# The S5 mixer's tables prepared by GpSimd instead of the vector engine

## The chip, the cores and the metric

The kernel runs on one core of a Trainium2 chip. The metric is the device time of one execution in microseconds (us). Engines are named as the profile names them: PE is the tensor engine, DVE the vector engine, ACT the scalar engine, POOL is GpSimd, SP the engine that issues nearly all transfers. Each engine works through its own list of instructions strictly in order; where an instruction needs another engine's result, it waits on a semaphore, and everything behind it on its engine waits too.

## The reference

The reference is a two-layer streaming encoder in float32, 512 tokens by 1024 channels. Each layer is a SwiGLU FFN (half weight), a mixer pair, and a second FFN:

```
x = x + 0.5 * _swiglu(h, ffn1_w_gate[layer], ffn1_w_up[layer], ffn1_w_down[layer])
...
y_a = _ssd_mixer(zxbcdt, ...)
y_b = _s5_mixer(u, s5_a_re[i], s5_a_im[i], s5_log_dt[i], s5_b_re[i], ...)
mixed = jnp.concatenate([y_a, y_b], axis=-1) @ even_w_out[i]
...
x = x + 0.5 * _swiglu(h, ffn2_w_gate[layer], ffn2_w_up[layer], ffn2_w_down[layer])
```

The S5 mixer of layer 0 is a complex diagonal recurrence in 32 groups of 16 channels with 64 states each. What it needs before it sees any token depends on parameters alone:

```
dt = jnp.exp(log_dt)[:, None]
mag = jnp.exp(dt * ar)
abar_re, abar_im = mag * jnp.cos(dt * ai), mag * jnp.sin(dt * ai)
den = ar * ar + ai * ai
f_re = ((abar_re - 1.0) * ar + abar_im * ai) / den
f_im = (abar_im * ar - (abar_re - 1.0) * ai) / den
bb_re = f_re[..., None] * br - f_im[..., None] * bi
```

The kernel turns the recurrence into products over chunks of eight tokens. For these it needs powers of `abar`, three matrices per group (inputs B, outputs G, direct term T), and rotation tables with the cosines, sines and decays of 64 chunk steps.

## The kernel before

Six stages follow each other: FFN f0, the even mixers, f1, f2, the odd mixers, f3. Tokens lie along the free dimension; every weight is a "unit" of 128x1024 numbers that SP loads into a `raw` tile. ACT rounds it into the upper half of a `whl` tile, DVE subtracts to get the lower half, and PE multiplies the unit in 24 products 128x512 (three per 128 rows of input: upper by upper, upper by lower, lower by upper). In f0 there are three `raw` and three `whl` tiles until the S5 preparation is done; the memory of the preparation then becomes more of them.

During f0 a generator, `s5_prepare`, computes the S5 tables beside the products. Its steps, with the tile names by which the profile and the listings know them:

- exponentials, sine and cosine (`ex`, `sc`; results `s5mag`, `s5sn`, `s5cs`),
- powers of abar (`s5pr`, `s5pi`, temporary `s5tm`), copies of them in other orders (`s5a`, `s5x`), the factors f (`s5fr`, `s5fi`, denominator `s5dn`), the scaled input matrices (`s5bc`, `s5bm`) and powers of the phase (`s5er`, `s5ei`, `s5erp`, `s5eip`),
- `tables(q)`, twice: the rotation tables `ct` (one buffer) with temporary `t`, sent to DRAM scratch `prm`,
- `gains_of_inputs(e)`, eight times: `bt` and `tc`, transposed by PE, copied by ACT into `bl`, sent to `prm`,
- `gains_of_outputs(e)`, eight times: `g` and `tb`, sent to `prm`; PE multiplies `g` by `s5bm`, ACT copies the result into `kt`, the diagonal term `td` is added, and eight small transfers send `kt` to `prm`.

The order of the work has two sources. For PE, DVE and ACT it is the order in which the program emits the instructions, and a class `Clock` estimates, while the program is written down, when each engine gets to what it has been given; a generator emits its next part when `on(engine, ...)` finds that engine near enough by this estimate. For POOL and SP the order is not the emission order: a scheduler of the framework places their instructions by its own estimate of times. So a transfer of `ct`, waiting for `ct` to be computed, may stand in SP's list ahead of a load of weights.

All instructions have the same source line in the profile, since a wrapper records each of them (L203); groups are told apart by tile names.

Of the kernel before, what the change touches and what calls it, by code (L numbers as in the profile page):

```python
# [14 lines left out]
PSUM = bass.MemoryType.PSUM  # L15
DRAM = bass.MemoryType.DRAM
# [3 lines left out]
D = 1024  # L20
# [17 lines left out]
# FFN: quads of four weight units (gate and up of two column tiles) in groups; a group's down products run  # L38
# between the pairs of the next group
# [4 lines left out]
# tiles: of all phases, and more of them in the FFNs  # L44
# [62 lines left out]
class Clock:  # L107
    """An estimate, while the program is written down, of when each engine gets to what it has been given."""
# [31 lines left out]
    @staticmethod  # L140
    def cost(eng, op, out, kw):
        n = max(out.free_size(), kw["in_"].free_size() if op == "tensor_reduce" else 0)
        if eng == "PE":
            if op == "transpose":
                return 0.12
            if kw["lhsT"].dtype == F32R:
                return max(0.11, 0.0025 + n / 2400)
            if out.partition_size() == 64:
                return 0.035 + n * 0.00084
            return max(0.21, 0.04 + n * 0.00168) if n < 512 else 0.86  # L150
        if eng == "ACT":
            return (0.2 if hasattr(kw.get("scale"), "space") or hasattr(kw.get("bias"), "space") else 0.09) + n * 0.00084
        one = op in ("tensor_scalar", "tensor_copy") and kw.get("in0", kw.get("in_")).space != PSUM
        ptr = any(hasattr(kw.get(k), "space") for k in ("scalar", "scalar1"))
        return (0.128 if ptr else 0.068) + n / (1920 if one else 960) * (1 if eng == "DVE" else 2)
# [59 lines left out]
class Ring:  # L215
    """Tiles of one kind, counted: taken when they are made and given back with their last reader."""
# [31 lines left out]
class Builder:  # L248
# [31 lines left out]
    # generators that emit their parts in turn with the main stream of products  # L280
# [34 lines left out]
    # waits in a generator until an engine could start on these operands without holding up others  # L315
# [14 lines left out]
    # counted tiles: a place is taken before the tile is made and left with its last reader  # L330
# [23 lines left out]
    # banks of PSUM  # L354
# [78 lines left out]
    # products that nothing reads keep the tensor engine's clock up while it waits  # L433
# [6 lines left out]
    # the mixers' small parameters  # L440
# [33 lines left out]
    # weight units come in the order of the plan, loaded and split ahead of their products  # L474
# [95 lines left out]
    # the lower part as minus the upper one plus the weights themselves, added by the DMA  # L570
# [44 lines left out]
    # RMS norm: x times the gains, split, goes into the products, and the rows' factors come after them  # L615
# [46 lines left out]
    # what the norm left; its factors may come later  # L662
# [11 lines left out]
    # two units, so that there is work while the last parts of h come in  # L674
# [34 lines left out]
    # what waits for the norm's factors  # L709
# [7 lines left out]
    # one unit of an output product into four banks; the last one finishes the banks one by one  # L717
# [23 lines left out]
    # the FFN, its gate and up products in seven block products for eight (Strassen's scheme in Winograd's form):  # L741
    # the blocks are two column tiles by two halves of D (weights) and two halves of D by two of the tokens
# [83 lines left out]
    # the last output products begin: what they finish goes on to the next norm  # L826
# [23 lines left out]
    # x, normalized, as float32 (from the split parts when x has gone on)  # L850
# [15 lines left out]
    # sums of blocks of the normalized x  # L866
    def blocks(self, h, gi, late):
        v = self.nc.vector
        lo, hi = slice(0, 512), slice(512, 1024)
        a, b = slice(0, 256), slice(256, 512)  # L870
        while not self.scaled():
            yield
        # the last ones stay until they can go in place of h, the others are made again
        hold = HOLD[late]
        again, kept = range(max(0, 4 - hold)), {}
# [27 lines left out]
        # the normalized x itself takes the place of what the unnormalized products read  # L903
# [29 lines left out]
    def pair(self, w, tag):  # L933
# [6 lines left out]
        # of two products in a bank, the one that is read first comes last: one engine at a time in a bank  # L940
# [30 lines left out]
    # up * silu(gate), split; how much of it is done: 1 the silu, 2 the product too  # L971
# [18 lines left out]
    # accurate functions on small tiles  # L990
# [51 lines left out]
    # parameters of the S5 mixer, per eighth of its groups, into DRAM scratch  # L1042
    def s5_prepare(self, pool):
# [24 lines left out]
        yield from self.on("DVE")  # L1068
# [23 lines left out]
        yield from self.on("DVE")  # L1092
# [7 lines left out]
        yield from self.on("DVE")  # L1100
        for j in range(8):
            n = 7 - j
            v.tensor_copy(out=x1[lo, :, j:j + 1], in_=pwr[lo, :, n:n + 1])
            v.tensor_copy(out=x1[hi, :, j:j + 1], in_=pwi[hi, :, n:n + 1])
            v.tensor_copy(out=x2[lo, :, j:j + 1], in_=a2[lo, :, n:n + 1])
            v.tensor_copy(out=x2[hi, :, j:j + 1], in_=pwr[hi, :, n:n + 1])
            if j % 2:
                yield from self.on("DVE")
# [6 lines left out]
        v.reciprocal(out=den, in_=den)  # L1115
# [10 lines left out]
        yield from self.on("DVE")  # L1126
# [7 lines left out]
        yield from self.on("DVE")  # L1134
        v.tensor_tensor(out=brr, in0=brr, in1=frb, op=ALU.mult)
        v.tensor_tensor(out=brr, in0=brr, in1=t16, op=ALU.subtract)
        yield from self.on("DVE")
        v.tensor_tensor(out=bri, in0=bri, in1=frb, op=ALU.mult)
        v.tensor_tensor(out=bri, in0=bri, in1=t17, op=ALU.add)
        yield from self.on("DVE")  # L1140
        v.tensor_copy(out=bmx[lo, 0:G], in_=brr[lo])
        v.tensor_copy(out=bmx[hi, 0:G], in_=bri[hi])
        yield from self.on("DVE")
        # powers of the unit phase: E, E^2, ... E^32
# [3 lines left out]
        for k in range(5):  # L1148
            cmul(er[:, :, k + 1], ei[:, :, k + 1], er[:, :, k], ei[:, :, k], er[:, :, k], ei[:, :, k], t1)
            yield from self.on("DVE")  # L1150
        # the same for pairs of groups, one in each half of the partitions
# [5 lines left out]
        yield from self.on("DVE")  # L1157
        # G, K and T0
        def gains_of_outputs(e):
# [13 lines left out]
            yield from self.on("DVE")  # L1173
            # K and T0, a group in each quarter of the partitions
# [13 lines left out]
            yield from self.on("DVE", kt)  # L1188
# [4 lines left out]
            for j in range(8):  # L1193
                nc.sync.dma_start(out=part(2)[16 * j:16 * j + 16], in_=kt[:, :, 112 - 16 * j:240 - 16 * j])
                if j % 4 == 3:
                    yield from self.on("DVE")

        # B
        def gains_of_inputs(e):
# [22 lines left out]
            yield from self.on("DVE")  # L1222

        # rotation tables and decay, for half of the groups
        def tables(q):
# [7 lines left out]
            for k in range(6):  # L1233
                n = 1 << k
                sh = [P, 8, n]
                cmul(c0[:, :, n:2 * n], s0[:, :, n:2 * n], c0[:, :, 0:n], s0[:, :, 0:n],
                     erp[:, qs, k:k + 1].to_broadcast(sh), eip[:, qs, k:k + 1].to_broadcast(sh), t3[:, :, 0:n])
                yield from self.on("DVE")
# [82 lines left out]
    def s5_quarter(self, q, ys):  # L1321
# [13 lines left out]
        # 2*gelu(y), split  # L1335
# [82 lines left out]
    # SSD  # L1418
# [81 lines left out]
    # o <- 2*o*sigmoid(2*o), by a silu as long as the activation engine has its table, or else by a tanh  # L1500
# [241 lines left out]
    def qk_norm(self, t, kq):  # L1742
# [32 lines left out]
        # per head: key parts and query parts, one over the other, for the exact products  # L1775
# [133 lines left out]
    def odd(self, then):  # L1909
# [4 lines left out]
        with tc.tile_pool(name=self.n("odd"), bufs=2) as p:  # L1914
# [13 lines left out]
            # v, token-major  # L1928
# [137 lines left out]
```

## Time and profile before

| what | value |
|---|---|
| timed runs (3) | 1830.42, 1833.75, 1837.24 us; median 1833.75 us |
| profiled execution | span 1837.6 us; nothing is shown of what lies around the span |
| PE busy | 1819.0 us, 99% of the span |
| DVE busy | 1429.3 us, 78%; from 20 to 200 us 159.67 of 180 us |
| ACT busy | 753.1 us, 41% |
| POOL busy | 16.6 us, 1%, 31 instructions |
| S5 preparation on DVE | first instruction at 20.11 us, last additions to `kt` at 192.0 us |

In the profile's rows, a group is given as engine, operation, tiles written and read, form and count, then busy time and mean duration, then the idle time before it and what ended that idle time. A timeline row gives the start, the busy time and the count of instructions merged, with idle time ahead in brackets. SPq is SP's transfer queue.

### The profile page before, as it was taken

To read this page: it belongs to the slowest core of one execution; us is meant where nothing else is said; L and a number is where in the kernel's file an instruction comes from. 1 tells how busy PE (TensorE), PEld (TensorE's weight loads), DVE (VectorE), ACT (ScalarE), POOL (GpSimd) and SP (SyncE) were. 2 spreads that over 40 slices of the span, in tenths; PEclk is the share of its full clock that TensorE was granted. 3 is DMA by queue.
4 is the path that set the end of the run, shared out by engine and by line. 5 is a ranking of instruction groups with operands and counts; after the bars stand their busy time and mean duration, and the time that the engine had idled before them with its cause. 6 is when DMAs were issued, how large, how long until landed. Compare 5 with 4: busy or idle time off the path is not lost.

```text
span 1837.6 us, 26795 instructions
## 1 busy us (share of the span) xinstructions
PE 1819.0 (99%) x10514; PEld 1574.3 (86%) x10514; DVE 1429.3 (78%) x2599; ACT 753.1 (41%) x1082; POOL 16.6 (1%) x31
## 2 busy tenths in 40 slices
PE   9999999999999999999999999999999999999999
PEld 7877888978878899999888999998876788999997
DVE  8989868778986888877688988866477578988864
ACT  4224423333664444333344443334455444434331
POOL 0000000000000000000000000000000000000000
PEclk9999999999999999999999999999998999999999
DMA  5246432347772323333422243342334321333331
GB/s 197 93 132 196 143 103 69 115 145 209 186 195 79 93 81 115 104 104 104 138 69 77 96 117 103 103 138 88 102 81 92 92 81 58 120 109 105 104 104 69
DMA packets 80749, 207.16 MB, mean 113 GB/s; under 512 B 18000, under 2 KB 30320, under 8 KB 79472
## 3 DMA queue, kind: packets, MB, share of 16 engines
q1 hardware_dynamic: 78032, 196.52, 34.2%
q0 software_dynamic: 2448, 8.91, 2.9%
q8 instruction: 83, 1.36, 0.3%
q14 instruction: 42, 0.34, 0.1%
q10 hardware_dynamic: 144, 0.02, 0.0%
HBM read 192.82 MB, written 12.60 MB: 112 GB/s over the span
## 4 chain that ended last, share of the span: by engine, by line
PE 88%; DVE 9%; issue 1%; DMA 1%; ACT 1%; SPq 0%; DVEq 0%; ACTq 0%
PE ps L203 88%; DVE whl L203 1%; DVE hg L203 1%; DMA ssb<-acsd 1%; DVE s_t L203 1%; DVE us L203 1%; DVE ex L203 1%; DVE ssb L203 0%; DVE acc L203 0%; DVE s5x L203 0%; ACT whl L203 0%; DVE sc L203 0%; DMA hg<-s5us 0%; DVE s_sc L203 0%; DVE x L203 0%
## 5 line engine op out<-in xcount | busy, mean ns | idle before, releaser
L203 PE MATMUL ps<-hg,whl 128*128 128x512 f32 (+1 forms) x8688 | 1616.6, 346 | 6.6 <-DVE hg L203 2.7
L203 PEld LDWEIGHTS ps<-hg,whl 128*128 128x128 f32 x8688 | 1379.6, 190 | 209.3 <-DVE hg L203 4.9
L203 ACT CAST whl<-raw 128x1024 fp32r<-128x1024 f32 x366 | 382.3, 1050 | 544.3 <-PE ps L203 324.5
L203 DVE TENSOR_TENSOR whl<-raw,whl 128x1024 fp32r<-128x1024 f32 x349 | 423.5, 1220 | 185.3 <-ACT whl L203 184.6
L203 DVE SCALAR_TENSOR_TENSOR x<-ps,x 128x512 f32<-128x512 f32 x128 | 86.8, 685 | 37.1 <-PE ps L203 35.5
L203 DVE TENSOR_TENSOR raw<-raw,raw 128x512 f32<-128x512 f32 (+1 forms) x182 | 111.2, 648 | 2.2
L203 ACT CAST hg<-us 128x512 fp32r<-128x512 f32 x88 | 52.0, 618 | 105.3 <-DVE us L203 105.0
L203 PE MATMUL ps<-hg,wh 128*128 128x256 f32 x624 | 83.4, 283 | 0.0
L203 ACT ACTIVATE gs<-gs 128x1024 f32<-128x1024 f32 x44 | 46.6, 1059 | 85.4 <-DVE gs L203 85.4
L203 PEld LDWEIGHTS ps<-hg,wh 128*128 128x128 f32 x624 | 78.6, 192 | 0.0
L203 ACT COPY p<-ps 128x256 f32<-128x256 f32 x52 | 19.3, 371 | 96.0 <-PE ps L203 76.1
L203 DVE TENSOR_TENSOR raw<-raw 128x512 f32<-128x512 f32 (+1 forms) x78 | 46.4, 595 | 15.5 <-DMA raw<-in_wgu_dram 15.3
L203 DVE TENSOR_TENSOR hg<-us,hg 128x512 fp32r<-128x512 f32 x88 | 57.7, 682 | 0.0
L203 DVE TENSOR_TENSOR us<-gs,us 128x1024 f32<-128x1024 f32 x44 | 53.6, 1217 | 0.4
L203 ACT ACTIVATE hg<-x,gains 128x512 fp32r<-128x512 f32 x48 | 33.6, 720 | 33.2 <-DVE x L203 30.4
L203 ACT CAST hg<-raw 128x512 fp32r<-128x512 f32 x58 | 34.1, 618 | 22.2 <-DVE raw L203 21.6
L203 DVE TENSOR_TENSOR hg<-raw,hg 128x512 fp32r<-128x512 f32 x58 | 38.0, 683 | 0.1
L203 DVE SCALAR_TENSOR_TENSOR hg<-x,gains,hg 128x512 fp32r<-128x512 f32 x48 | 34.9, 743 | 2.7 <-ACT hg L203 2.7
L203 DVE TENSOR_TENSOR wh<-raw,wh 128x512 fp32r<-128x512 f32 x52 | 35.5, 683 | 0.0
L203 DVE TENSOR_TENSOR us<-ps,rsB 128x512 f32<-128x512 f32 x40 | 28.9, 721 | 4.6 <-PE ps L203 4.5
L203 ACT CAST wh<-raw 128x512 fp32r<-128x512 f32 x52 | 32.0, 616 | 0.0
L203 DVE TENSOR_TENSOR acc<-acc,sq 128x512 f32<-128x512 f32 x42 | 28.8, 685 | 0.9
(263 smaller groups left out, 1112.4 us busy)
## 6 DMA issues: line engine op xcount, KB each, us to landing
raw<-in_wgu_dram SPq DMA_DIRECT2D x176, 512.0 KB, 3.5
raw<-in_wdn_dram SPq DMA_DIRECT2D x88, 512.0 KB, 3.6
raw<-in_wev_dram SPq DMA_DIRECT2D x16, 512.0 KB, 3.7
prm<-prm SPq DMA_DIRECT2D x8, 1024.0 KB, 6.6
raw<-in_wod_dram SPq DMA_DIRECT2D x12, 512.0 KB, 3.4
raw<-in_wevo_dram SPq DMA_DIRECT2D x8, 512.0 KB, 6.3
raw<-in_wodo_dram SPq DMA_DIRECT2D x8, 512.0 KB, 6.5
x<-in_xT_dram SPq DMA_DIRECT2D x8, 256.0 KB, 5.2
```

The costliest lines, as they stand in the source:

```text
L203: r = f(*args, **kw)
```

## The change

Everything in `s5_prepare` behind the exponentials and the sine is issued to POOL instead of DVE: powers, copies, factors, tables and gains, 272 instructions in all (206 `tensor_tensor`, 45 copies, 4 multiplications by a constant, 17 memsets). One instruction of that part stays on DVE: the reciprocal of `s5dn`. The `on("DVE")` conditions of this part become `on("POOL")`, and the `Clock` estimate for POOL goes from 2 to 2.5 times DVE's time per element. Comments are removed. Nothing else is changed.

```diff
@@ Clock.cost
-        return (0.128 if ptr else 0.068) + n / (1920 if one else 960) * (1 if eng == "DVE" else 2)
+        return (0.128 if ptr else 0.068) + n / (1920 if one else 960) * (1 if eng == "DVE" else 2.5)
@@ s5_prepare
         self.sincos_small(pool, sn, cs, th, [2, G])
-        yield from self.on("DVE")
+
+        v = nc.gpsimd
+        yield from self.on("POOL")
         m8 = tl("s5m8", [G])
         v.tensor_tensor(out=m8, in0=mag, in1=mag, op=ALU.mult)
...
-        yield from self.on("DVE")
+        yield from self.on("POOL")
...
-        v.reciprocal(out=den, in_=den)
+        nc.vector.reciprocal(out=den, in_=den)
...
-            yield from self.on("DVE", kt)
+            yield from self.on("POOL", kt)
...
```

The lists of instructions show three places. The first is SP's list around the first loads of down-projection weights (`in_wdn`). In the kernel before, the fifteenth to eighteenth weight units (raw_724, raw_778, raw_819, raw_868) stand ahead of every transfer of a table:

```order
L203 DMA raw_665<-in_wgu_dram 128x1024
L203 DMA raw_724<-in_wdn_dram 128x1024
L203 DMA raw_778<-in_wgu_dram 128x1024
L203 DMA raw_819<-in_wgu_dram 128x1024
L203 DMA raw_868<-in_wdn_dram 128x1024
L203 DMA raw_921<-in_wgu_dram 128x1024
L203 DMA prm_139<-g_107_971 128x4x128
L203 DMA raw_992<-in_wgu_dram 128x1024
```

In the changed kernel, the same fifteenth, sixteenth and seventeenth units are raw_757, raw_807 and raw_865, and the transfers of both rotation tables (ct_870 for the first half of the groups, ct_1132 for the second) stand between and ahead of them:

```order
L203 DMA raw_713<-in_wgu_dram 128x1024
L203 DMA prm_139<-ct_870 128x3x128
...
L203 DMA prm_142<-ct_870 128x3x128
L203 DMA raw_757<-in_wdn_dram 128x1024
L203 DMA prm_143<-ct_1132 128x128
...
L203 DMA raw_807<-in_wgu_dram 128x1024
L203 DMA prm_143<-ct_1132 128x3x128
...
L203 DMA prm_146<-ct_1132 128x3x128
L203 DMA raw_865<-in_wgu_dram 128x1024
L203 DMA raw_922<-in_wdn_dram 128x1024
```

What moved: both tables' transfers went from behind the eighteenth unit to places ahead of the fifteenth and the seventeenth.

The second place is POOL's list, where the first input gains (bt_884) end, then the first table, and the second table begins in the same buffer:

```order
L203 TENSOR_TENSOR bt_884<-s5bc,s5x_588 128x512
L203 TENSOR_TENSOR tc_886<-s5bc,s5x_589 128x512
L203 TENSOR_TENSOR t_95_871<-ct_870,s5erp 128x8x16
L203 TENSOR_TENSOR bt_884<-bt_884,tc_886 128x512
L203 TENSOR_TENSOR ct_870<-ct_870,t_95_871 128x8x16
...
L203 TENSOR_TENSOR ct_870<-ct_870,t_95_871 128x8x32
L203 MEMSET ct_1132 128x8 x3
L203 COPY ct_1132<-s5m8p 128x8x63
```

What moved: all of these stood in DVE's list before, between the products' own work, and POOL's list had only two masks there.

The third place is PE's list in the changed kernel, in the fourteenth unit (whl_849) and behind it, where PE first needs a result of POOL:

```order
L203 MATMUL ps_950<-hg_135,whl_849 128x512 x3
L203 MATMUL ps_950<-hg_154,whl_849 128x512 x3
L203 MATMUL ps_964<-ident,bt_884 128x128 x4
L203 MATMUL ps_950<-hg_166,whl_849 128x512 x3
...
L203 MATMUL ps_991<-hg_575,whl_915 128x512 x3
...
L203 MATMUL ps_1051<-hg_135,whl_954 128x512 x3
...
L203 MATMUL ps_1087<-hg_135,whl_995 128x512 x3
```

What moved: the transposes of the first `bt` stood 60 products later before (300 products 128x512 behind the broadcast of the norm's factors, `rqy`, against 240 now). whl_915, whl_954 and whl_995 are the units of raw_757, raw_807 and raw_865; whl_995 begins 306 products 128x512 and one group of four transposes behind that broadcast.

More of the change, by code (lines that the diff above doesn't have):

```diff
@@ L1099, in s5_prepare @@
         v.tensor_scalar(out=a2[hi], in0=pwr[hi], scalar1=-1.0, scalar2=None, op0=ALU.mult)
-        yield from self.on("DVE")
+        yield from self.on("POOL")
         for j in range(8):
@@ L1107, in s5_prepare @@
             if j % 2:
-                yield from self.on("DVE")
+                yield from self.on("POOL")
         fr, fi, den = tl("s5fr", [G]), tl("s5fi", [G]), tl("s5dn", [G])
@@ L1125, in s5_prepare @@
         v.tensor_tensor(out=fi, in0=fi, in1=den, op=ALU.mult)
-        yield from self.on("DVE")
+        yield from self.on("POOL")
         bsh = [P, G, 16]
@@ L1133, in s5_prepare @@
         v.tensor_tensor(out=t17, in0=brr, in1=fib, op=ALU.mult)
-        yield from self.on("DVE")
+        yield from self.on("POOL")
         v.tensor_tensor(out=brr, in0=brr, in1=frb, op=ALU.mult)
         v.tensor_tensor(out=brr, in0=brr, in1=t16, op=ALU.subtract)
-        yield from self.on("DVE")
+        yield from self.on("POOL")
         v.tensor_tensor(out=bri, in0=bri, in1=frb, op=ALU.mult)
         v.tensor_tensor(out=bri, in0=bri, in1=t17, op=ALU.add)
-        yield from self.on("DVE")
+        yield from self.on("POOL")
         v.tensor_copy(out=bmx[lo, 0:G], in_=brr[lo])
         v.tensor_copy(out=bmx[hi, 0:G], in_=bri[hi])
-        yield from self.on("DVE")
+        yield from self.on("POOL")
         er, ei = tl("s5er", [G, 6]), tl("s5ei", [G, 6])
@@ L1149, in s5_prepare @@
             cmul(er[:, :, k + 1], ei[:, :, k + 1], er[:, :, k], ei[:, :, k], er[:, :, k], ei[:, :, k], t1)
-            yield from self.on("DVE")
+            yield from self.on("POOL")
         erp, eip, m8p = tl("s5erp", [G // 2, 6]), tl("s5eip", [G // 2, 6]), tl("s5m8p", [G // 2])
@@ L1156, in s5_prepare @@
             v.tensor_copy(out=m8p[r], in_=m8[r].rearrange("p (g b) -> p g b", b=2)[:, :, b])
-        yield from self.on("DVE")
+        yield from self.on("POOL")
         def gains_of_outputs(e):
@@ L1172, in gains_of_outputs @@
             nc.sync.dma_start(out=part(1), in_=g1[:, :, 1:9].rearrange("p g j i -> p g (j i)"))
-            yield from self.on("DVE")
+            yield from self.on("POOL")
             yield from self.on("PE", g1, bmx, ps=1)
@@ L1195, in gains_of_outputs @@
                 if j % 4 == 3:
-                    yield from self.on("DVE")
+                    yield from self.on("POOL")
         def gains_of_inputs(e):
@@ L1221, in gains_of_inputs @@
             nc.sync.dma_start(out=prm[:, 0:512], in_=bcal)
-            yield from self.on("DVE")
+            yield from self.on("POOL")
         def tables(q):
@@ L1237, in tables @@
                      erp[:, qs, k:k + 1].to_broadcast(sh), eip[:, qs, k:k + 1].to_broadcast(sh), t3[:, :, 0:n])
-                yield from self.on("DVE")
+                yield from self.on("POOL")
             v.tensor_copy(out=m0[:, :, 1:64], in_=m8p[:, qs].unsqueeze(2).to_broadcast([P, 8, 63]))
```

## The prediction

> **What bounds the kernel now.** I read the page's first part, then PE's timeline in f0, then the stretches around the one gap in it.
>
> ```profile
> PE 1819.0 (99%) x10514; PEld 1574.3 (86%) x10514; DVE 1429.3 (78%) x2599; ACT 753.1 (41%) x1082; POOL 16.6 (1%) x31
> PE 88%; DVE 9%; issue 1%; DMA 1%; ACT 1%; SPq 0%; DVEq 0%; ACTq 0%
> 20.00:200.00 180.00, 177.22 (x837) 143.40 (x836) 159.67 (x445) 58.19 (x92) 0.00 (x0) 0.98 0.47 137
> ```
>
> PE sets the end: it is busy 99% of the span and holds 88% of the chain of waits. In 20 to 200 us, where the preparation runs, PE (second number) works 177.22 of 180 us, DVE (fourth) 159.67, POOL none. So taking work from DVE is worth only what PE loses to DVE in that stretch:
>
> ```profile
> 28.35 68.28 PE L203 MATMUL ps<-hg,whl 128*128 128x512 f32 x300
> 96.47 0.60 PE L203 MATMUL ps<-ident,bt 128*128 128x128 f32 x4
> 101.09 0.66 PE L203 MATMUL ps<-g,s5bm 128*32 128x128 f32 x8 [2.78 <-DVE us L203]
> 98.00:100.00 2.00, 0.32 (x2) 1.00 0.74 273
> 100.00:102.00 2.00, 0.91 (x9) 0.54 0.50 131
> 102.00:104.00 2.00, 2.00 (x6) 0.50 0.91 342
> 104.00:106.00 2.00, 2.00 (x6) 0.50 0.04 14
> 106.00:108.00 2.00, 2.00 (x8) 0.75 0.60 131
> 108.00:110.00 2.00, 2.00 (x11) 1.00 0.35 139
> ```
>
> PE waits once, 2.78 us for DVE's `us`. The granted clock (the number behind the count) then falls to 0.54, 0.50, 0.50 and 0.75 for 2 us each, which costs 2 x (0.46 + 0.50 + 0.50 + 0.25) = 3.4 us. These 6.2 us are all that a free DVE can bring in the preparation.
>
> **The change, part by part.** What leaves DVE was off PE's path but for those 6.2 us: a gain of **-6.2 us** if the gap goes.
>
> What comes to POOL has to be fast enough for two lists that run in fixed order. SP's list now holds the loads of units 15 (raw_757) and 16, 17 (raw_807, raw_865) behind the transfers of the rotation tables, so these weights cannot be asked for before POOL has made the tables. That is the path that I cost.
>
> When PE wants unit 17: by the first PE row, 300 products take 68.28 us, 0.2276 us each. Unit 17 begins 306 products and 4 transposes (0.60) behind 28.35 us, so at 28.35 + 69.6 + 0.6 = 98.6 us.
>
> When POOL can deliver it: POOL starts on the powers when DVE has `s5cs`, and nothing before that point in DVE's list has changed. The rows that bear on POOL's prices:
>
> ```profile
> 40.17 0.20 DVE L203 TENSOR_SCALAR s5cs<-sc 128x64 f32<-128x64 f32 x1
> L203 POOL TENSOR_SCALAR_AFFINE_SELECT ident<-ones 128x128 f32<-128x128 f32 x1 | 0.3, 287 | 0.6 <-DVE ones L203 0.6
> 1.16 0.29 POOL L203 TENSOR_SCALAR_AFFINE_SELECT ident<-ones 128x128 f32<-128x128 f32 x1 [0.63 <-DVE ones L203]
> 1.40 0.29 POOL L203 TENSOR_SCALAR_AFFINE_SELECT tri<-ones 128x128 f32<-128x128 f32 x1
> L203 POOL MEMSET strip<- 64x64 f32 x8 | 1.2, 144 | 748.1 <-DVE acc L203 740.8 <-DMA strip<-in_strip_dram 7.3
> L203 DVE TENSOR_TENSOR g<-s5bc,s5a 128x576 f32<-128x576 f32 x8 | 6.0, 747 | 0.0
> L203 DVE TENSOR_TENSOR tc<-s5bc,s5x 128x512 f32<-128x512 f32 x8 | 5.4, 678 | 0.0
> L203 DVE TENSOR_TENSOR ct<-ct,s5erp 128x256 f32<-128x256 f32 x2 | 0.8, 418 | 0.0
> L203 DVE TENSOR_TENSOR s5er<-s5er 128x32 f32<-128x32 f32 x5 | 1.1, 217 | 0.0
> L203 DVE MEMSET ct<- 128x8 f32 x6 | 0.2, 65 | 4.5 <-DMA prm<-ct 4.5
> ```
>
> No row shows POOL with two inputs. The nearest is the mask, one input of 128 columns: 287 ns long, the next one 0.24 us later, so 0.24/128 = 1.87 ns per column. Bounds: below, DVE's own durations (217 ns for 32 columns, 418 for 256, 678 for 512, 747 for 576); above, one full pass per input, 3.74 ns per column. I take the middle, counting accesses: the mask reads once and writes once, a two-input operation reads twice and writes once, so 1.5 x 1.87 = 2.8 ns per column (1.44 us for 512, 1.62 for 576, 0.72 for 256, 0.36 for 128). Nothing goes below 287 ns, since most instructions wait for the one ahead; memsets take 144.
>
> From the first product with `s5cs` to the end of the first table POOL's list holds 150 instructions: 109 small ones (109 x 0.287 = 31.3), 4 of 288 and 2 of 512 columns with one input (2.2 + 1.9), and with two inputs 12 of 128 (4.3), 6 of 256 (4.3), 10 of 512 (14.4) and 7 of 576 (11.3): 69.7 us. First table ready at 40.4 + 69.7 = 110.1 us. The table has one buffer, and DVE in the last row above waited 4.5 us for the transfers out of it; so does POOL. The second table is 40 instructions: 3 memsets, a copy of 504 (0.94), 24 small (6.9), 6 of 128 (2.2), 6 of 256 (4.3): 14.8 us. Ready at 129.4 us.
>
> Then SP and the split:
>
> ```profile
> 113.89 3.62 SPq L203 DMA_DIRECT2D prm<-ct  x7
> raw<-in_wgu_dram SPq DMA_DIRECT2D x176, 512.0 KB, 3.5
> L203 ACT CAST whl<-raw 128x1024 fp32r<-128x1024 f32 x366 | 382.3, 1050 | 544.3 <-PE ps L203 324.5
> L203 DVE TENSOR_TENSOR whl<-raw,whl 128x1024 fp32r<-128x1024 f32 x349 | 423.5, 1220 | 185.3 <-ACT whl L203 184.6
> ```
>
> Four issues at 3.62/7 = 0.52 us (2.1), landing 3.5, the cast 1.05: PE can begin unit 17 at 136.0 us, 37.4 us late. The third product needs DVE's 1.22 us, two products cover 0.46: **+0.8**. The clock falls after a wait longer than the one above: **+3.4**, of which nothing can be caught up, since PE has no slack later. The earlier waits lie inside the same delay: the first `bt` (23.6 us of POOL work after it until 129.4, plus the hold, so about 104) against PE's 28.35 + 240 x 0.2276 = 83.0, and unit 15 (110.1 + 2.1 + 3.6 + 1.05 = 116.9) against 87.7. DVE's reciprocal waits for `s5dn` at about 60 us where DVE arrives near 50; behind it the split of unit 11 ends near 61 us and PE wants it at 65. That is covered by the units split ahead; were POOL 4 us later, it would only be an earlier part of the same wait.
>
> Behind unit 17, POOL has per eighth of the groups 3 x 1.62 + 3 x 1.44 + 3 x 0.287 = 10.0 us, and PE's list has an eighth every 10.9 us (two units of 24 x 0.2276): covered, narrowly. From then on all lists are as before.
>
> Sum: 37.4 + 0.8 + 3.4 - 6.2 = **+35.4 us**. The profiled span is 1837.6 us, 3.9 above the median of the runs, and what lies around it is not shown; the sum goes from 1837.6 to 1873.0, and by the runs' median from 1833.75 to **1869 us**.
>
> The Trainium skill prices this directly: its GPSIMD Engine Reference, section 3.1, gives 4497 ns for a two-input add of 2048 columns on GpSimd and 2293 on VectorE. That estimate of 2.2 ns per column is between my lower passes, and by it the sum would be some 9 us smaller; no row here shows such an operation.
>
> **Rivals.**
>
> *A: POOL and DVE exclude each other.* If a DVE operation with two inputs in SBUF and a POOL operation cannot run together, POOL's work is stretched by DVE's. For the 16 units ahead, up to 10 splits at 1.22, 3 products `us<-gs,us` at 1.22 and 6 splits `hg<-us,hg` at 0.68 fall into POOL's stretch:
>
> ```profile
> L203 DVE TENSOR_TENSOR us<-gs,us 128x1024 f32<-128x1024 f32 x44 | 53.6, 1217 | 0.4
> L203 DVE TENSOR_TENSOR hg<-us,hg 128x512 fp32r<-128x512 f32 x88 | 57.7, 682 | 0.0
> ```
>
> That is 12.2 + 3.7 + 4.1 = 20 us more: 1889. Each later eighth then takes 10.0 + about 4.6 us against 10.9, up to 18 us more over five: 1907. Neither for nor against: in this trace POOL never computes beside DVE but for the 144 ns memsets, which read nothing. The Trainium skill's SBUF page ("SBUF — State Buffer", section "Who interferes with whom") says just this: the second read port is one lock, and whichever comes second blocks. By that rule this rival holds.
>
> *B: two full passes.* At 3.74 ns per column the two stretches are 81.1 and 16.9 us: 13.5 more, 1883, and up to 13 us in the later eighths, 1896. Against it: most of the work is small instructions, which do not change.
>
> *C: POOL as fast as DVE, not slower.* Its instructions overlap (masks start 0.24 us apart at 0.287 long). With DVE's durations the stretches are 43.7 and 9.6 us; unit 17 is ready at 40.4 + 53.3 + 4.5 + 6.65 = 104.9, 6.3 late: +6.3 + 0.8 + 3.4 - 6.2 = +4, 1838. It decides at 47 us for the 190 instructions (98.6 - 40.4 - 4.5 - 6.65); below that the 6.2 us are won, 1828. Against it: 47/190 is 247 ns each, less than the one POOL row with an input.
>
> *D: one pass.* 1.87 ns per column: 58.8 and 12.9 us, 12.8 less: 1856. It is the lower part of my own case.
>
> **How the numbers follow.** My case with D (POOL between one pass and 1.5, SP's order deciding): 0.50, 1856 to 1883 around 1869. A: 0.28. B: 0.10. C: 0.12, nearly all of it within 0.5% (9 us, about what a measurement of this kernel can tell). The range for 8 in 10 goes from C's upper end to A's: 1840 to 1905. Faster by over 0.5% needs under 1824.6, more than the 6.2 us that there are: 0.02. Same 0.10, slower 0.88.
>
> **What would show it.** PE's first long wait at about 83 us, on POOL's `bt`; SP's `raw` loads of units 15 and 17 directly behind `prm<-ct`; PE waiting for `whl` until about 136 us, the clock at 0.5 behind it, and no `us` gap near 98. DVE's `RECIPROCAL` waits for POOL. POOL's `tc` at 1.44 us speaks for my price, at 0.96 for D, 1.9 for B; durations that grow where DVE's splits run, for A. I am wrong in kind if unit 17's load comes out of SP by 92 us, or if the time is lost elsewhere than in f0.

## The result: 2.35% slower, and the profile after

The changed kernel takes 1874.0 us (median of 4 runs, 1872.2 to 1884.3), the kernel before 1833.45 us in runs of the same sitting: 40.6 us more, a ratio of 1.0235 with a 95% interval of 1.0201 to 1.0269. The forecast was 1869 us, 1840 to 1905, and slower.

The profiled execution of the changed kernel took 1872.8 us with a span of 1871.1. Busy time and the chain of waits, from its page:

```profile
PE 1817.7 (97%) x10514; PEld 1572.6 (84%) x10514; DVE 1371.6 (73%) x2327; ACT 752.4 (40%) x1082; POOL 169.2 (9%) x303
PE 85%; DVE 5%; POOL 5%; DMA 2%; ACT 1%; issue 1%; SPq 0%; POOLq 0%; ACTq 0%; DVEq 0%
```

VectorE (DVE) is busy 58 us less and GpSimd (POOL) 153 us more. The two figures do not give the price of the moved work directly, since three groups of two-input operations that stayed on VectorE now take 17 us longer in all (the splits `whl<-raw,whl` 435.0 us, before 423.5; `hg<-us,hg` 62.0, before 57.7; `us<-gs,us` 54.4, before 53.6). So some 74 us of work left VectorE, and GpSimd takes about twice as long for it. TensorE (PE) is no longer busy throughout. Where it waited, from its timeline (start, us, then in brackets the idle time before and what ended it):

```profile
72.51 20.20 PE L203 MATMUL ps<-hg,whl 128*128 128x512 f32 x76 [6.40 <-DVE whl L203]
110.22 1.11 PE L203 MATMUL ps<-ident,bt 128*128 128x128 f32 x4 [17.51 <-POOL bt L203]
...
122.72 4.08 PE L203 MATMUL ps<-hg,whl 128*128 128x512 f32 x9 [5.13 <-ACT whl L203]
128.77 10.77 PE L203 MATMUL ps<-hg,whl 128*128 128x512 f32 x39 [1.98 <-ACT bl L203]
146.21 14.51 PE L203 MATMUL ps<-hg,whl 128*128 128x512 f32 x54 [6.67 <-ACT whl L203]
```

All of it lies between 66 and 146 us. The 2.78 us gap on `us` near 98 us is gone, as is any wait after 146 us that the kernel before did not have. The row at 146.21 is unit 17: the forecast had TensorE wanting it at 98.6 us, so it comes 47.6 us late. SyncE's list shows why it and unit 15 come so late (the queue's issues in order of time):

```profile
115.47 2.03 SPq L203 DMA_DIRECT2D prm<-ct  x4
117.60 0.46 SPq L203 DMA_DIRECT2D raw<-in_wdn_dram  x1
...
138.27 2.03 SPq L203 DMA_DIRECT2D prm<-ct  x4
140.40 0.46 SPq L203 DMA_DIRECT2D raw<-in_wgu_dram  x1
```

Unit 15 is issued right behind the first table (117.60), unit 17 right behind the second (140.40). Each `prm<-ct` waits until GpSimd has the table; the weights behind it have nothing to wait for but their place in the list.

Then GpSimd's own rows. The first block shows prices where VectorE is idle or is itself the one that waits, called free below (32 columns, a broadcast and a contiguous operation of 512, the same of 576); the second an operation of 32 columns beside a long one of VectorE (`us<-gs,us`, 73.16 to 74.80 us); the third is the hold of the table's one buffer:

```profile
98.07 0.25 POOL L203 TENSOR_TENSOR s5fi<-s5fi,s5dn 128x32 f32<-128x32 f32 x1
107.54 1.04 POOL L203 TENSOR_TENSOR tc<-s5bc,s5x 128x512 f32<-128x512 f32 x1
108.92 1.25 POOL L203 TENSOR_TENSOR bt<-bt,tc 128x512 f32<-128x512 f32 x1
65.96 1.16 POOL L203 TENSOR_TENSOR g<-s5bc,s5a 128x576 f32<-128x576 f32 x1
69.98 1.39 POOL L203 TENSOR_TENSOR g<-g,tb 128x576 f32<-128x576 f32 x1
...
73.66 1.27 POOL L203 TENSOR_TENSOR s5fi<-s5fi,s5tm 128x32 f32<-128x32 f32 x1
...
120.68 0.19 POOL L203 MEMSET ct<- 128x8 f32 x3 [5.24 <-DMA prm<-ct]
```

Free, GpSimd works at 2.0 ns per column with a broadcast input (1.04 us / 512) and 2.4 with two contiguous ones. Beside VectorE's operations with two inputs an operation of 0.25 us can take 1.27 us. And it goes the other way too. VectorE's rows near 67 us:

```profile
67.37 0.35 DVE L203 RECIPROCAL s5dn<-s5dn 128x32 f32<-128x32 f32 x1 [15.04 <-POOL s5dn L203]
67.64 4.82 DVE L203 TENSOR_TENSOR whl<-raw,whl 128x1024 fp32r<-128x1024 f32 x1
```

VectorE waits 15 us for `s5dn`, and the split behind it then takes 4.82 us instead of 1.22, while GpSimd runs three operations of 576 columns and two of 32 between them without a gap (67.31 to 71.37 us). TensorE's 6.40 us at 66 to 72.5 us are these two rows.

### The profile page after: what moved, and what is told of

Same layout as the page of the kernel before. It is cut to its first block, busy times and chain, and to the rows that moved or that the text cites. A ratio compares the mean times of both kernels' runs of the same rounds, so it can differ in the third digit from the quotient of the medians.

```text
span 1871.1 us, 26825 instructions
## 1 busy us (share of the span) xinstructions
PE 1817.7 (97%) x10514; PEld 1572.6 (84%) x10514; DVE 1371.6 (73%) x2327; ACT 752.4 (40%) x1082; POOL 169.2 (9%) x303
## 4 chain that ended last, share of the span: by engine, by line
PE 85%; DVE 5%; POOL 5%; DMA 2%; ACT 1%; issue 1%; SPq 0%; POOLq 0%; ACTq 0%; DVEq 0%
PE ps L203 85%; POOL ct L203 1%; DVE hg L203 1%; DVE whl L203 1%; DMA ssb<-acsd 1%; POOL s5tm L203 1%; DVE ex L203 1%; DVE s_t L203 1%; POOL t L203 0%; DMA raw<-in_wglu_dram 0%; ACT whl L203 0%; POOL s5x L203 0%; SPq L203 0%; DVE ssb L203 0%; ACT hg L203 0%
## 5 line engine op out<-in xcount | busy, mean ns | idle before, releaser
L203 DVE TENSOR_TENSOR whl<-raw,whl 128x1024 fp32r<-128x1024 f32 x349 | 435.0, 1254 | 270.5 <-ACT whl L203 269.8
L203 DVE TENSOR_TENSOR hg<-us,hg 128x512 fp32r<-128x512 f32 x88 | 62.0, 734 | 2.1 <-ACT hg L203 2.1
L203 DVE TENSOR_TENSOR us<-gs,us 128x1024 f32<-128x1024 f32 x44 | 54.4, 1237 | 1.0 <-ACT gs L203 0.3
```

The lines of the kernel that those rows point to most:

```text
L203: r = f(*args, **kw)
```

## The experiments

All times are medians and stand against runs of the kernel before on the same chip (1831.3, 1831.45, 1830.9 and 1830.75 us in the four sittings). The change itself (1874.0 us) was timed only beside the 1833.45 us above, so a difference between it and an experiment is sure to about 2 us. Two theories run through them. The **order theory** is that of the forecast: lists that run in order wait for GpSimd. The **throughput theory** is the forecast's rival A: GpSimd and VectorE take time from each other.

### e1: the tables' transfers behind the loads

```
+            while len(self.loads) < (20, 30)[q]:
+                yield
...
-                nc.sync.dma_start(out=dst[:, 0:3], in_=ct...)
+                d = nc.sync.dma_start(out=dst[:, 0:3], in_=ct...)
+                self.after(d, self.loads[-1])
```

> Edit: the change, with the transfers of the two rotation tables put behind the weight load that was written down last when 20 (first table) and 30 (second table) loads had been, so that no load of units 15 to 20 stands behind a transfer that waits for GpSimd. GpSimd's work is the same. Order theory (two lists wait for GpSimd: TensorE's own, for the first gains of the inputs, 17.5 us at 110 us; then SyncE's, which holds unit 17 until 146 us): only the second wait goes. The first stays, since GpSimd is no faster: TensorE reaches the transposes at about 83 us and gets them at about 110, 27 us late; less the 6.2 us that are won, plus about 4 for the clock: 1856 to 1863 us, and unit 17 directly behind. Rival, throughput theory (GpSimd and VectorE take time from each other, and TensorE waits for what VectorE and GpSimd make, whatever the order of the loads): 1870 to 1876 us, the waits move to another place but their sum stays.

Measured: 1859.2 us (1858.6 to 1862.2), ratio 1.0148 (1.0123 to 1.0173). TensorE's timeline and SyncE's queue:

```profile
113.65 1.11 PE L203 MATMUL ps<-ident,bt 128*128 128x128 f32 x4 [21.92 <-POOL bt L203]
92.91 0.33 SPq L203 DMA_DIRECT2D raw<-in_wgu_dram  x1
134.84 4.32 SPq L203 DMA_DIRECT2D prm<-ct  x8
```

The loads now leave SyncE up to 92.9 us, the tables at 134.8, and unit 17 is no longer waited for. What is left is the wait for the first `bt` and, ahead of it, one of 6.43 us at 72 us on the split that VectorE makes late. So of the 43 us by which the change lies above this sitting's runs before, SyncE's hold is about 15 (13, if each kernel is taken against the runs before of its own sitting), and the wait for the first gains, with what lies ahead of it in the list and the clock behind it, 28. The order theory's number and place are both right.

### e2: transposes later, loads still held

```
+        if eng == "POOL":
+            return 0.25 + n / 960 * 4
```

> Edit: the change, with GpSimd's instructions priced at 0.25 us + 4/960 us per column in the planner, in place of 0.068 us + 2.5/960, so that TensorE's transposes of the gains are written down later: the first behind 552 products in place of 240. SyncE's list is not helped: the transfers of the first table now stand ahead of unit 14, those of the second ahead of units 15 and 16. Order theory: TensorE's wait for the first gains goes, but the load of unit 16 still leaves SyncE behind the second table, at about 140 us, and can be used at about 146, where TensorE wants it at 28.35 + 282 x 0.2276 + 0.6 = 93: 53 us late, less 6.2, plus 3.4, in sum slower than the change, 1876 to 1886 us. Rival (what costs is that TensorE waits for the gains, and the loads only follow): with that wait gone 1830 to 1848 us.

Measured: 1925.7 us (1920.7 to 1928.3), ratio 1.0499 (1.0465 to 1.0532): slower than either theory said. TensorE's timeline, and its largest sum of waits:

```profile
79.76 13.26 PE L205 MATMUL ps<-hg,whl 128*128 128x512 f32 x48 [8.71 <-ACT whl L205]
109.87 13.51 PE L205 MATMUL ps<-hg,whl 128*128 128x512 f32 x48 [16.85 <-ACT whl L205]
132.51 1.22 PE L205 MATMUL ps<-hg,whl 128*128 128x512 f32 x2 [9.13 <-ACT whl L205]
PE ps L205 <- ACT hg L205: 38.8, 5, 32.3
```

The wait for `bt` at 83 us is gone, and the loads alone bring 34.7 us of waits by 132 us: the rival (only the gains cost) is wrong. What comes later neither theory had: two waits of 9.6 us together for later `bt` near 330 us, and 32.3 us in one wait for `hg` at the FFN's end. e3 to e5 are about the latter.

### e3 and e4: later transposes and free loads

e3 is the edits of e1 and e2 together. e4 adds, on VectorE and ahead of GpSimd's work:

```
+        v.tensor_tensor(out=den, in0=ar, in1=ar, op=ALU.mult)
+        v.tensor_tensor(out=di, in0=ai, in1=ai, op=ALU.mult)
+        v.tensor_tensor(out=den, in0=den, in1=di, op=ALU.add)
+        v.reciprocal(out=den, in_=den)
```

> Edit: both of the last two edits together, later transposes and the tables' transfers behind the loads. GpSimd does all the work of the change. Order theory: no list waits for GpSimd any more but VectorE's reciprocal (6.4 us at TensorE in the change, there hidden in a later wait). So the 40 us go nearly whole: -6.2 for the gap of before, +6.4 and 2 to 3 for the clock: 1832 to 1840 us. Throughput theory: GpSimd's 130 us of work still stretch VectorE's operations with two inputs, and TensorE waits for its splits: 1845 to 1875 us.

> Edit: as before it, and the denominator |a|^2 and its reciprocal made by VectorE ahead of GpSimd's work (four operations of 32 columns), so that VectorE never waits for GpSimd. Order theory: TensorE's 6.4 us wait at 66 us goes, and what is left is what a freer VectorE brings: 1827 to 1835 us, 4 to 9 us below the one before it. If the two engines' exclusion alone starved that split (4.82 us for one of 1.22), the wait stays and the two are equal.

Measured: e3 1899.5 us (1892.8 to 1905.8), ratio 1.0364; e4 1902.8 us (1899.9 to 1906.5), ratio 1.0384. Both expectations of the order theory were missed by over 55 us; e3 also lies 24 us above the throughput theory's range. TensorE's timeline of e3, then of e4 (a wait of 8.93 us at 80.4 us in e3 is not shown):

```profile
367.77 0.58 PE L205 MATMUL ps<-hg,whl 128*128 128x256 f32 x1 [33.24 <-ACT hg L205]
```

```profile
80.41 1.22 PE L205 MATMUL ps<-hg,whl 128*128 128x512 f32 x2 [9.28 <-ACT whl L205]
95.66 54.67 PE L205 MATMUL ps<-hg,whl 128*128 128x512 f32 x226 [4.46 <-ACT whl L205]
```

The waits for the first `bt` and for units 15 to 17 are gone (two waits for later `bt`, 9 us together, stand near 300 us in both). Three things came in their place. First, units 12 and 13 stand in SyncE's list behind the transfers of the first two gains of the outputs, `prm<-g`, which also wait for GpSimd; that is the 9 us. Second, e4's denominator moved GpSimd's list so that the second of these transfers came 12 us later, and unit 13 with it: the mended reciprocal gave nothing. Third, the 33 us at the FFN's end: the planner, told that GpSimd is dear, wrote the preparation's last products close to the end of the FFN, and the sums of blocks of x that the block products read are only begun when the preparation is over, since they use its memory. **The preparation has a second due date, its end.**

### e5: all of these lists free

As e4, with another price and the first transfers of the gains behind 18 loads:

```
-            return 0.25 + n / 960 * 4
+            return 0.4 + n / 960 * 1.6
...
+            while len(self.loads) < 18:
+                yield
             yield from self.on("DMA", g1)
-            nc.sync.dma_start(out=part(1), in_=g1...)
+            d = nc.sync.dma_start(out=part(1), in_=g1...)
+            self.after(d, self.loads[-1])
```

> Edit: as e4 (transposes later, the tables' transfers behind the loads, denominator on VectorE), with two sizes mended that e3 and e4 showed: the transfers of the first gains of the outputs also go behind 18 loads (they held unit 12 until 75 us in e3 and e4, TensorE waited 9 us), and GpSimd is priced at 0.4 us + 1.6/960 us per column, so that its first transposes come behind 402 products and its last about 165 products earlier than in e4, well ahead of the FFN's end (in e3 and e4 TensorE lost 33 us there). Order theory: with no list behind GpSimd, all the work of the change costs nothing: no wait of over 2 us in the preparation, 1827 to 1838 us, and the loss of e3 and e4 at the FFN's end goes too. Throughput theory: VectorE and GpSimd still stretch each other, 1845 us or more.

Measured: 1854.4 us (1852.3 to 1854.6), ratio 1.0128 (1.0105 to 1.0151). TensorE's two waits, and VectorE's rows ahead of the first:

```profile
99.31 29.92 PE L205 MATMUL ps<-hg,whl 128*128 128x512 f32 x118 [6.38 <-DVE whl L205]
330.10 0.58 PE L205 MATMUL ps<-hg,whl 128*128 128x256 f32 x1 [15.53 <-ACT hg L205]
77.66 8.55 DVE L205 TENSOR_TENSOR whl<-raw,whl 128x1024 fp32r<-128x1024 f32 x1
...
86.91 2.80 DVE L205 TENSOR_TENSOR us<-gs,us 128x1024 f32<-128x1024 f32 x1
90.40 6.41 DVE L205 TENSOR_TENSOR hg<-us,hg 128x512 fp32r<-128x512 f32 x2 [0.69 <-ACT hg L205]
96.73 2.52 DVE L205 TENSOR_TENSOR whl<-raw,whl 128x1024 fp32r<-128x1024 f32 x1
```

No wait for GpSimd and none for a load is left, and the kernel is still 23 us slower than before. The order theory's 1827 to 1838 us is wrong: it is not true that all this work costs nothing once no list stands behind it. 15.5 us are the second due date. In 255 to 335 us VectorE makes 16 of the normalized rows `raw<-hg` in e5 and 4 in the kernel before (groups of that stretch, before and e5):

```profile
L203 DVE TENSOR_TENSOR raw<-hg 128x512 f32<-128x512 f32 x4 | 2.7, 684 | 0.0
```

```profile
L205 DVE TENSOR_TENSOR raw<-hg 128x512 f32<-128x512 f32 x16 | 11.0, 686 | 0.0
```

The other 6.4 us come at the end of a run of VectorE's operations that are stretched one after the other: a split of 8.55 us in place of 1.22, 2.80 us in place of 1.22, two `hg<-us,hg` of 6.41 us in place of 1.29, and 2.52 us for the split that TensorE waits for. VectorE waits for nothing of GpSimd's ahead of them. This is the throughput theory's mechanism, and its number (1845 us or more) is met.

### e6: the denominator alone

The four operations that e4 adds, in place of those of GpSimd and the reciprocal behind them, and nothing else.

> Edit: the change, with the denominator and its reciprocal made by VectorE ahead of GpSimd's work, and nothing else. TensorE's first wait (6.4 us at 66 us, on the split that VectorE made late) goes. Order theory: that wait lay inside the later ones, so the next wait, for the first gains, grows by as much, from 17.5 to about 24 us, and the time is that of the change, 1870 to 1877 us. If the waits add up: 1866 to 1869 us.

Measured: 1874.2 us (1873.6 to 1874.6), ratio 1.0239: the time of the change. But the waits are others:

```profile
122.30 4.62 PE L203 MATMUL ps<-hg,whl 128*128 128x512 f32 x9 [13.40 <-ACT whl L203]
145.23 14.88 PE L203 MATMUL ps<-hg,whl 128*128 128x512 f32 x51 [8.00 <-ACT whl L203]
```

The 6.4 us wait is gone, and the one for `bt` too, which I expected to grow; units 12 (9.1 us at 80 us), 15 and 17 are what TensorE now waits for longest. Yet unit 17 is reached at 145.2 us, in the change at 146.2. Waits along one list do not add up: the last one sets the time, and taking an earlier one away moves it into the next.

### e7, e8, e12: the two engines beside each other

To the kernel before, whose VectorE keeps all its work, 200 operations of GpSimd are added from the sines on, that nothing reads. e7 adds this; e8 has `nc.gpsimd.memset(zz, 0.0)` in its place, e12 `out=zz[i % 4]`:

```
+        for i in range(200):
+            nc.gpsimd.tensor_tensor(out=zz, in0=cs[:, 0], in1=sn[:, 0], op=ALU.mult)
```

> Edit: the kernel before, with 200 multiplications of 32 columns with two inputs in SBUF added on GpSimd from the sines on (40 us), whose result nothing reads; VectorE keeps all its own work. Measures whether the two engines exclude each other. If they do: GpSimd's operations last 0.25 us alone and 1.2 us or more beside a split of VectorE (1.22 us), and VectorE's splits get longer than their 1.22 us in that stretch; VectorE is busy 160 of 180 us there, so TensorE starts to wait for it: 3 to 15 us slower. If GpSimd is only slow by itself: all 200 near one duration, VectorE's durations as before, same time.

> Edit: as e7, but the 200 operations are memsets of 32 columns, which read nothing. If the exclusion is one of reads from SBUF, or of operations with two inputs: VectorE's splits stay at 1.22 us, and the time is that of before within 0.3%. If any GpSimd instruction slows VectorE: as e7.

> Edit: as e7 (the kernel before, 200 idle multiplications of 32 columns with two inputs on GpSimd from 40 us on), but the products go into four tiles in turn, so that an operation no longer waits for the one just ahead of it. In e7 each did, which left 0.08 us between two, VectorE's splits stayed near 1.22 us and GpSimd's operations were stretched to 0.5 us apart. In the change, e5 and e9, operations of GpSimd that don't depend on each other ran without a gap, and a split of VectorE took 4.8 to 8.6 us. Gap theory (VectorE gets its second input only where GpSimd leaves a gap): here GpSimd's stream passes in about 200 x 0.21 = 42 us, VectorE's splits and other operations with two inputs last 3 us to many times that, TensorE waits for them, 15 to 40 us slower than before. Size theory (it is GpSimd's long operations of 512 and 576 columns that hold VectorE off): as e7, within 0.3% of before.

Measured: e7 1832.4 us, ratio 1.0009 (0.9993 to 1.0026); e8 1832.2 us, ratio 1.0003 (0.9982 to 1.0024); e12 1835.0 us, ratio 1.0028 (1.0013 to 1.0042). For e7, e8 and e12 in turn, GpSimd's stream (for e7 and e12 duration least, median, most in ns, then first and last start; for e8 its timeline) and VectorE's splits beside it (between 36 and 110 us, in e8 up to 42 us; busy us, then mean in ns):

```profile
L203 POOL TENSOR_TENSOR s5zz<-s5cs,s5sn x200: 251/255/1597, 40.9 to 140.3; 128x32 f32<-128x32 f32 x100
L203 DVE TENSOR_TENSOR whl<-raw,whl 128x1024 fp32r<-128x1024 f32 x13 | 16.1, 1247 | 0.0
```

```profile
1.81 36.04 POOL L203 MEMSET s5zz<- 128x32 f32 x197
L203 DVE TENSOR_TENSOR whl<-raw,whl 128x1024 fp32r<-128x1024 f32 x8 | 9.7, 1222 | 1.3 <-ACT whl L203 1.2
```

```profile
L203 POOL TENSOR_TENSOR s5zz<-s5cs,s5sn x200: 241/252/1255, 40.5 to 109.9; 128x32 f32<-128x32 f32 x100
L203 DVE TENSOR_TENSOR whl<-raw,whl 128x1024 fp32r<-128x1024 f32 x12 | 15.1, 1261 | 0.0
```

The engines exclude each other: an operation of GpSimd that reads lasts 0.25 us or, beside a split, up to 1.3 to 1.6, and 200 of them take 99 us in e7 and 70 in e12 where they would take some 50. VectorE loses only 2 to 4% on its splits (1218 ns in that stretch of the kernel before). The memsets of e8 wait for nothing and so ran from the start on, up to 38 us, not in the stretch that I had meant; beside them the splits are as long as in the same stretch of the kernel before (1222 ns against 1221), so that instructions which read nothing cost VectorE nothing there. So with small operations it is mainly GpSimd that pays. VectorE's loss still reaches TensorE: between 20 and 200 us TensorE waits for it 6.2 us in e7 and 7.8 in e12, in the kernel before 2.8. Of the 3 to 15 us that e7 was expected to lose, its times show none clear of noise (the interval ends at 1.0026, 4.8 us). e12 sets aside the explanation that VectorE gets in only where GpSimd leaves a gap: without the waits between them, the small operations still cost only 0.28% (about 5 us). Long stalls of VectorE, 4.8 to 8.6 us, were only seen beside GpSimd's operations of 512 and 576 columns, with a few of 32 between them. e11 below agrees: its GpSimd has no operation with two inputs over 256 columns, and between 20 and 340 us no operation of VectorE lasts over 1.64 us. That points to the size; a stream of long operations by itself was not tried.

The Trainium skill says, on its page "SBUF — State Buffer", section "Who interferes with whom", that an operation of VectorE with two inputs in SBUF contends with a GpSimd instruction that reads SBUF and not with one that only writes, and that the other one is blocked for the whole instruction. e7 and e8 agree (up to 1597 ns against 251 beside a busy VectorE; splits of 1222 ns beside memsets). That VectorE can be kept out through several instructions in a row, as in e5 and e9, the page does not say.

### e9: tables on VectorE, the rest late

As e5, with the price 0.4 + 2/960 and, in the rotation tables and their complex products:

```
-                yield from self.on("POOL")
+                yield from self.on("DVE")
-            v.tensor_copy(out=m0[:, :, 1:64], in_=m8p...)
+            nc.vector.tensor_copy(out=m0[:, :, 1:64], in_=m8p...)
```

> Edit: as e5 (first transfers of the gains behind 18 loads, denominator on VectorE, GpSimd priced higher: 0.4 us + 2/960 us per column), but the two rotation tables go back to VectorE. e5 lost 15.5 us at the FFN's end, since the sums for the block products are only begun when the preparation has ended (at 252 us of TensorE's list, 191 us before the change), and 6.4 us at 93 us. Here GpSimd has 80 operations less, the first transposes stand behind 405 products (120 us) and the last products of the preparation behind about 813 (213 us). Order theory with the preparation's end as second due date: no wait of over 2 us in the preparation or at the FFN's end, 1826 to 1836 us, as before or little better. If the end at 213 us is still too late for the sums: 1836 to 1846 us.

Measured: 1854.3 us (1853.2 to 1854.8), ratio 1.0132 (1.0116 to 1.0147). The wait at the FFN's end is gone, though the preparation's last products came at 225 us and not at 213; the time is not, and both expected ranges are missed. TensorE's two waits, and VectorE and GpSimd ahead of the second (the `ct` rows are the second table):

```profile
98.34 29.06 PE L205 MATMUL ps<-hg,whl 128*128 128x512 f32 x121 [5.58 <-DVE whl L205]
158.73 2.08 PE L205 MATMUL ps<-hg,whl 128*128 128x512 f32 x4 [8.00 <-DVE whl L205]
141.70 0.12 DVE L205 MEMSET ct<- 128x8 f32 x3 [6.70 <-DMA prm<-g]
...
143.27 7.14 DVE L205 TENSOR_TENSOR ct<-ct,t 128x8 f32<-128x8 f32 x1
```

```profile
143.42 1.16 POOL L205 TENSOR_TENSOR g<-s5bc,s5a 128x576 f32<-128x576 f32 x1
...
149.33 1.05 POOL L205 TENSOR_TENSOR tc<-s5bc,s5x 128x512 f32<-128x512 f32 x1
```

An operation of VectorE on 8 columns lasts 7.14 us, from the first of six long operations of GpSimd that run without a gap (two of them are shown) to the end of the sixth. Ahead of TensorE's first wait stand operations of VectorE stretched in the same way (a split of 8.10 us at 77 us). Ahead of the second, VectorE had also stood still for 6.70 us at the second table's first memset, by the profile for a transfer. By the FFN's end e9 is 12 us behind the kernel before (its first `hg,wh` products start at 329.3 us, in the kernel before at 317.1) and 15 behind e8 (314.2), which does the work of the kernel before; at the end of the span it is 23 us behind e8. For most of these 8 us the trace shows the granted clock: from 480 to 560 us, in the mixers, it costs e9 13.6 us (0.74, 1.00, 0.87 and 0.71 in four windows of 20 us), and e8 1.8 us there and 5.2 us near 1370 us, where e9 loses none. Why it falls there is open.

### e10 and e11: each half alone

e10 is the change with the second edit of e9 alone (tables on VectorE). e11 is its counterpart: `v = nc.vector` again for all but the tables, which stay on GpSimd.

> Edit: the change, with only the rotation tables (80 of GpSimd's operations) given back to VectorE; the rest stays on GpSimd and the planner's prices as in the change. SyncE's list then has the loads of units 15 to 18 ahead of the tables' transfers. Order theory: no wait for a load; TensorE still reaches the first transposes at 83 us, and GpSimd, without the table operations that it had done by then (9 to 10 us), has the gains at about 101: 18 us late, +4 for the clock, -6.2: 1845 to 1854 us. If the cost goes by the amount of work on GpSimd alone (80 of 300 operations): about 1863 us.

> Edit: the other half alone: only the rotation tables on GpSimd, all else on VectorE as before. TensorE's transposes then wait for VectorE as before, and the tables' transfers stand behind the load of unit 18. Order theory: GpSimd starts on the tables only when VectorE has the powers of the phase, and some loads behind the first table may come late, but units 15 to 18 don't: 1826 to 1842 us. If any work on GpSimd beside a busy VectorE costs its time: 1845 us or more.

Measured: e10 1859.1 us (1856.2 to 1865.0), ratio 1.0169 (1.0146 to 1.0192); e11 1852.1 us (1850.5 to 1854.5), ratio 1.0121 (1.0106 to 1.0136). For e10 TensorE's waits:

```profile
101.72 1.12 PE L203 MATMUL ps<-ident,bt 128*128 128x128 f32 x4 [11.57 <-POOL bt L203]
122.06 1.09 PE L203 MATMUL ps<-ident,bt 128*128 128x128 f32 x4 [5.13 <-DVE us L203]
```

The first gains come at 101.7 us, as the order theory had it (101); but VectorE, which now also makes the tables beside GpSimd, is late at 122 us, which it had not. Both numbers are missed: 1859.1 lies between the 1854 of the order theory and the 1863 of the other. For e11 TensorE, VectorE and SyncE's queue:

```profile
120.27 0.65 PE L203 MATMUL ps<-g,s5bm 128*32 128x128 f32 x8 [7.02 <-DVE g L203]
117.91 0.76 DVE L203 TENSOR_TENSOR g<-s5bc,s5a 128x576 f32<-128x576 f32 x1 [9.48 <-DMA prm<-g]
92.17 22.50 SPq L203 DMA_DIRECT2D prm<-ct  x5
```

No weight is late in e11. But SyncE stands at the table's transfers from 92 to 114.7 us, the transfer of the gains `g` stands behind them, and VectorE waits 9.5 us for the buffer that this transfer is to empty. The same comes again at 138 us: VectorE waits 7.93 us for `kt`'s buffer behind the second table's transfers, and TensorE 6.81 us for `bt`. It is the order theory's mechanism through another list than I had looked at, but the time is the one that was expected if any work on GpSimd beside a busy VectorE costs time, and exclusion has its part in it: the first table lasts 24.6 us on GpSimd (89.66 to 114.28 us), where even the second table of the change lasted 17.5. These runs do not separate the two. The halves cost 28 and 21 us, together 49, and the whole 43 against the same runs: they overlap in part, as in e6.

No version tried is faster than the kernel before.

## Why the prediction was right, step by step

**What bounds the kernel, and the 6.2 us that a free VectorE can bring:** right in kind. Some 74 us of work left VectorE, the gap on `us` is gone, and nothing else was won. The size is that of one execution. e8, which does the work of the kernel before and idle memsets on GpSimd beside it, also waits 2.81 us for `us`, but its granted clock stays at 1.00 from 94 to 114 us (0.83 in the kernel before). There the gap costs 2.8 us; the 3.4 us of clock behind it do not come every time.

**SyncE's list and unit 17:** right in kind and place. The load left behind the second table at 140.40 us, the forecast had 131.5; e1 took the hold away and got 15 us back. The part ahead of it, the first `bt` at 104 us, came at 110.2, and the wait for it, with the 6.4 us ahead of it and the clock, is the other 28 us in e1. (The 104 us follow from 20.9 us of work behind `bt`, 6.1 for the rest of the first table and 14.8 for the second; the forecast's 23.6 is a slip.)

**GpSimd's price, 2.8 ns per column:** too high, and made good by what was left out. Free, it was 1.04 to 1.25 us for 512 columns (1.44 in the forecast), 1.16 to 1.39 for 576 (1.62), 0.22 to 0.36 for the small ones (0.287): nearer to rival D's pass of 1.87 ns than to 2.8. With these prices the stretch would take about 60 us, where the forecast had 69.7. It took from 41.0 to 115.4 us, 74.4. Of the difference, some 12 us are instructions stretched beyond their free duration, an estimate of what VectorE's operations took from GpSimd; the rest are mostly gaps between instructions. That the price and the missing exclusion nearly cancel is luck. **Rival A, exclusion, was true as a mechanism** and belonged into the sum, with D's price; as a rival on top of 2.8 ns it gave 1889. The estimate of 2.2 ns per column from the Trainium skill's "GPSIMD Engine Reference", section 3.1, by which the forecast did not sum, was nearer than my middle: the rows here give 2.0 to 2.4 ns. The lock that the Trainium skill's "SBUF — State Buffer" states in "Who interferes with whom" is borne out by the stretched rows.

**The hold of the one buffer, 4.5 us:** 5.24. **The second table, 14.8 us:** 17.5 (120.68 to 138.2), the same two errors, here without cancelling. **From the second table to unit 17, 6.65 us:** 8.0 (138.2 to 146.21).

**The clock, 3.4 us behind the wait, and 0.8 for the split:** about 2.0 and 0.3. Windows of 2 and 4 us (start, length, then the busy times; the clock stands behind the last count):

```profile
146.00:148.00 2.00, 1.75 (x3) 1.00 (x4) 1.81 (x3) 1.20 (x2) 0.00 (x0) 0.50 0.93 370
148.00:152.00 4.00, 4.00 (x15) 3.16 (x14) 2.97 (x4) 1.04 (x1) 0.00 (x0) 0.76 0.63 185
```

2 x 0.50 + 4 x 0.24 = 2.0 us, and TensorE is idle 0.25 of the first 2 us, the split's part. With the measured terms the sum is 47.6 + 0.3 + 2.0 - 6.2 = 43.7 us. At the FFN's end TensorE was 44.5 us behind the kernel before (the run of 159 products begins at 333.05 us, before at 288.57). Against e8, whose gap cost 2.8 us, the sum is 47.1 us, and TensorE was 47.3 us behind (e8's run begins at 285.73 us). At the end of the span 41.5 us of these are left (1871.1 and 1829.6 us), near the 40.6 of the medians. Most of the 5.8 us that come back are the granted clock in the mixers: from 380 to 1480 us it costs e8 7.0 us (mostly 0.81 and 0.93 in two windows of 20 us from 1360 us) and the changed kernel 1.8. It differs from execution to execution of the same work (from 1340 to 1480 us 13.6 us in the kernel before, 5.2 in e8, 1.6 in e7), and why is open.

**VectorE's reciprocal, "covered":** wrong. It began at 67.4 us, not 60, since GpSimd's list had other work of 576 columns ahead of `s5dn`, and the split behind it took 4.8 us; TensorE waited 6.4. That this cost nothing in the end (the forecast's "only an earlier part of the same wait") is right by e6.

**The later eighths, covered narrowly:** right, no wait for GpSimd after 146 us.

So the forecast was 5 us low: unit 17 came 10.2 us later than it had it (5.3 from the first table, 0.7 from the hold, 2.8 from the second table, 1.3 behind it), the clock and the split cost 1.9 us less, and some 3 us came back later. Its mechanism stands: lists that run in order wait for GpSimd. Its price and the exclusion that it left to a rival were mis-sized in opposite directions.

## What to carry to other kernels

When work moves to another engine, follow the lists that run in order behind its results before pricing it: a transfer that waits holds every load queued behind it, and its buffer holds the engine that fills it. Waits along one list do not add up; the last one sets the time, so mending one of three can bring nothing (e6), and mending all three can uncover a due date that the work had met by accident (e3 to e5). And GpSimd beside a VectorE that is busy with two-input operations was no second VectorE here: small operations got slower themselves, and beside runs of long ones VectorE stood still.

## What the runs showed that I had not expected

- **Who pays for the exclusion changes with the operations.** With 32 columns GpSimd mainly pays (0.25 us becomes up to 1.3 to 1.6) and a split of VectorE goes from 1218 to 1247 or 1261 ns. Beside runs of 512 and 576 columns VectorE pays: splits of 4.82, 8.10 and 8.55 us in place of 1.22, and 7.14 us for an operation on 8 columns. It was kept out through six instructions in a row in e9 and seven in e5 (the split of 8.55 us), not one. The size of the operations fits all these runs, but it was not varied alone, and why VectorE is not let in between two long ones is open.
- **A freer VectorE did not help anywhere.** In the change it is busy 58 us less than before, in e5 45, and in e5 TensorE still waits 15.5 us for sums that VectorE makes: what counts there is when its work may begin, not how much of it there is.
